# A two-block transformer kernel: a second triangular solve moved into the Fourier tables' place, and a head's work cut into nine pieces between projections

## The chip, the cores and the metric

The kernel is written for Trainium2 and runs on one core of one chip, as one program. The metric is the device time of that program in microseconds (us): the median of three runs. Beside it stands the profile of one execution, taken by the hardware profiler.

The engines meant below are PE (TensorE, matrix products and transposes), ACT (ScalarE), DVE (VectorE), POOL (GpSimd) and SP, the queue that issues nearly all transfers between device memory and on-chip memory. Each works through its own list of instructions in order, and waits at an instruction until what it needs is there.

## What is computed

All data is float32, 1024 tokens of width 1024. A first block (a gated linear recurrence, a short convolution and a pooling branch) hands its output to a second block. That one has a mixer of two branches, then a mixture of 64 experts. The change touches the second block's mixer alone:

```python
proj = rms_norm(h) @ w_in                 # Fourier input, q, k, v, z, a/b, gate_f, gate_d
y_f  = real(fft2(f_in, axes=(1, 3))) @ w_fourier
q, k, v = silu(depthwise_conv(qkv, width 5))       # 8 heads of 128
# per chunk of 64 tokens and head, forward and backward in time:
decay = exp(min(g[:, None] - g[None, :], 0)) on the lower triangle
a_mat = strict_lower((k * beta) @ k.T * decay)
t_mat = inverse(eye + a_mat)                       # triangular solve
qk    = lower(q @ k.T * decay)
# delta rule over the chunks with t_mat, qk, q, k, v and a state per head
y_d   = (rms_norm(o) * silu(z)) @ w_delta
out   = (sigmoid(gate_f) * y_f + sigmoid(gate_d) * y_d) @ w_out
```

## The kernel before, in words

**Products.** A float32 product is made of three passes over values that are split into a high and a low part (`mm3`, whose matmuls stand at lines 195 to 197). A block of weights arrives as `wr` (512 KB); ACT writes its high part `wh` (line 172) and POOL its low part `wl` (line 173).

**Order.** A framework's scheduler makes one ordered list per engine out of the program text; `tc.issue_after(x)` adds that what follows comes behind instruction x on x's engine. Tiles of a pool rotate over `bufs` buffers, so a writer waits until the reader of the buffer's last content is done.

**The heads** (lines 1125 to 1146, from about 1205 us to 1640 us of the profiled execution). For each of 8 heads, `channels` makes one of k, q, v: 72 matmuls for each of three column groups (348, 346, 346), evicted by ACT as `pr` (line 990), a convolution of width 5 on ACT and DVE (lines 994 and 996), then Silu. While head h is projected, head h-1 is finished: `token_rows` transposes k and q on PE (line 1024) and takes their norms on ACT, `value_rows` transposes v, `gram_meta` and `gram` form k k^T and q k^T (line 1093), multiply them by decays and store the results. The decays come from `gb`, cumulative log gates that a transfer copies out of the scratch `GR` to all 128 partitions (line 1003, `decays_in`): DVE subtracts (lines 1069 and 1082), ACT takes the exponent (lines 1071 and 1084). Two buffers in PSUM serve all these transposes (`m`), and two hold `gb` for each direction. The program text has `token_rows` whole behind the first projection and so on; the scheduler interleaves as its own rules have it.

**The tables.** Six loads `tr` (line 1122) bring the discrete Fourier tables, each is split by ACT and POOL (lines 172 and 173) into tiles `th`, `tl`. The text names one per head.

**Fourier and first solve** (1641 to 1773 us). PE transforms while DVE runs the first 38 of 62 steps of the solve of X0 (lines 438 and 440, forward direction, 128 systems of 64x64 side by side).

**Gate loop** (1773 to 1898 us). For n = 0 to 15, PE makes a half of gate_f and of the Fourier branch's output, and DVE multiplies the two (`mul`, line 1282). Between these DVE does the last 24 steps of the first solve, four to a half, in n = 0 to 5. Then ACT turns the solved X0 over (`inverse_out`, line 1208), X1 is loaded into the same place, and its solve (lines 421 and 423) goes on, seven steps to a half, and then alone.

**Tail** (1898 to 2009 us). PE makes six halves of z gates and ten of `gate_d`, 24 matmuls each, evicted by ACT (line 1349 for `gate_d`). When X1 is solved, ACT turns it over as well. Then the pools of the solves are closed, and the delta rule over chunks begins (first matmul at line 1375).

Of the kernel before, what the change touches and what calls it, by code (L numbers as in the profile page):

```python
# [11 lines left out]
F32 = mybir.dt.float32  # L12
# [97 lines left out]
INV0S, INV0 = 38, 6  # L110
# [22 lines left out]
def body(ctx, tc, A):  # L133
# [778 lines left out]
    with ExitStack() as cg:  # L912
# [66 lines left out]
        KQs_, vs_, sks, gbs = {}, {}, {}, {}  # L979

        def channels(h, j, m):

            if j == 0:
                KQs_[h] = pg.tile([P, 2, T2], F32, name="KQ", bufs=2)
            w = w_k if m == 8 else win2.get(512 + m * P)
            pr = pg.tile([P, T2 + 4], F32, name="pr", bufs=2)
            pool_e.memset(pr[:, 0:2], 0.0)
            pool_e.memset(pr[:, T2 + 2:], 0.0)
            for c0, n in CH2:
                act.activation(pr[:, 2 + c0:2 + c0 + n], q_k.pop() if q_k else proj2(w, c0, n), AF.Copy)  # L990
            if j == 2:
# [5 lines left out]
            act.activation(y, y, AF.Silu)  # L997
# [8 lines left out]
        def token_rows(h):  # L1006
# [5 lines left out]
            for j in range(2):  # L1012
# [7 lines left out]
                for gq in range(2):  # L1020
                    q = psm.tile([P, 4, P], F32, name="m")
                    for i in range(4):
                        c = 4 * gq + i
                        pe.transpose(q[:, i, :], KQ[:, j, 16 + c * P:16 + (c + 1) * P], ident)
                    for i in range(4):
                        act.activation(jk, q[:, i, :], AF.Square, accum_out=ss[:, j, 1 + 4 * gq + i:2 + 4 * gq + i])
                    if j == 0:
                        o = pg.tile([P, 4, P], F32, name="kv", bufs=3)
                        act.activation(o, q, AF.Copy)
                        sp.dma_start(KVs[4 * gq:4 * gq + 4, :, h, 0, :].rearrange("c p n -> p c n"), o)  # L1030
            for j in range(2):
                sp.dma_start(KQs[:, :, h, j, :].rearrange("c p t -> p c t"),
                             KQ[:, j, 16:].rearrange("p (c t) -> p c t", t=P))
# [7 lines left out]
            for d_ in range(2):  # L1041
                dve.tensor_mul(bp[:, d_, :, h], beta[:, d_, :, h], rq[:, 0])
                dve.tensor_scalar(nbp[:, d_, :, h], bp[:, d_, :, h], -1.0, None, op0=OP.mult)

        def value_rows(h):
# [6 lines left out]
            for gq in range(2):  # L1052
# [8 lines left out]
                paced[0] = sp.dma_start(KVs[4 * gq:4 * gq + 4, :, h, 1, :].rearrange("c p n -> p c n"), o)  # L1061

# [12 lines left out]
        def gram(h, gq):  # L1075
            KQ, grb = KQs_[h], gbs[h]
            dm = []
            for d_ in range(2):
# [6 lines left out]
                dm.append(t)  # L1085
            at = [pg.tile([P, 4, P], F32, name=f"at{d_}") for d_ in range(2)]
            qt = [pg.tile([P, 4, P], F32, name=f"qt{d_}") for d_ in range(2)]
            for i2 in range(2):
# [5 lines left out]
                for d_ in range(2):  # L1094
                    for i in range(2):
# [5 lines left out]
                                      dm[d_][:, 2 * i2:2 * i2 + 2], op=OP.mult)  # L1101
            cs_ = slice(4 * gq, 4 * gq + 4)
            for d_ in range(2):
# [5 lines left out]
                sp.dma_start(ov, at[d_][0:64, :, 64:128] if d_ == 0 else at[d_][64:128, :, 0:64])  # L1109

        tabs = [[pft.tile([KF, 6, NT], F32R, name=f"t{c}{j}") for c in "hl"] for j in range(2)]
# [13 lines left out]
        for h in range(H + 1):  # L1125
            if 0 < h < H:
                decays_in(h)
            if h < H:
                channels(h, 0, 8 + h)
                table_piece(h) if h < 7 else None  # L1130
            with tc.issue_after(mm[0].ins):
                if h == 0:
                    gates_a()
                else:
                    token_rows(h - 1)
            if h < H:
                channels(h, 1, h)
            if h == 0:
                with tc.issue_after(mm[0].ins):
                    gates_b()  # L1140
                decays_in(0)
            if h:
                value_rows(h - 1)
                gram_meta(h - 1)
                gram(h - 1, 0)
            if h < H:
                channels(h, 2, 16 + h)
            if h:
                gram(h - 1, 1)
# [45 lines left out]
    def inverse_in(d_):  # L1195
        X = pi.tile([P, 64, 64], F32, name="X")
        sp.dma_start(X, N2[d_])
        return X, pi.tile([P, 1024], F32, name="t", bufs=2)
# [61 lines left out]
    cff.close()  # L1260

    with ExitStack() as cf:
# [10 lines left out]
        for d in range(KT):  # L1273
            wg = win2.get(4640 + d * P)
            wp = wfo.get(d * P)
            for half, tt in enumerate(HALF):
# [9 lines left out]
                with tc.issue_after(mul.ins):  # L1286
                    if n < INV0:
                        run(solve, -(-(62 - INV0S) // INV0))
                    if n == INV0 - 1:
                        ones(X0)  # L1290
                    if n > INV0:
                        run(solve, 7)
                if n == INV0:
                    with tc.issue_after(sent.ins), tc.issue_after(gate.ins):
                        inverse_out(0, X0)
                        X1_, t1_ = inverse_in(1)
                    solve = solve_lower(X1_, 64, t1_)
    run(solve)
    ones(X1_)
    for h in range(5, H):  # L1300
        z_gate(h)
        if h == 6:
            with tc.issue_after(gated[0].ins):
                inverse_out(1, X1_)
            cpi.close()
# [865 lines left out]
```

## Time and profile before

| | us |
|---|---|
| three runs | 3086.24, 3081.46, 3084.51 |
| median | 3084.51 |
| the profiled execution, its own time | 3079.72 |
| its span in the trace | 3078.0 |
| PE busy | 2795.7 (91%) |
| DVE, ACT, POOL busy | 1518.6, 1051.5, 881.1 |

Times inside the trace are counted from the span's start. An engine's busy time is not yet its cost: what matters is where PE, the busiest engine, stands idle or runs at a lower clock, and which instruction ends each such pause. "Idle before, releaser" in the rows says how long an engine stood before an instruction and what let it go on.

### The profile page before, as it was taken

What the parts mean: (1) busy time and instruction counts of PE and PEld (TensorE: products, weight loads), DVE (VectorE), ACT (ScalarE), POOL (GpSimd) and SP (SyncE); (2) the same over time, 40 slices, a digit from 0 to 9 for tenths busy, and PEclk for the clock granted to TensorE, in tenths of its full rate; (3) what the DMA queues carried; (4) which work ended last, traced back from release to release, by engine and by line L of the source; (5) the groups of instructions that cost most, each with busy time, mean ns of one, the idle gap of its engine ahead of it and who ended that gap; (6) DMA issues with size and microseconds to landing.
All of it is one profiled execution on the core that took longest, in us unless ns stands there. A gap on an engine that the chain in (4) does not pass through costs nothing.

```text
span 3078.0 us, 42949 instructions
## 1 busy us (share of the span) xinstructions
PE 2795.7 (91%) x16109; PEld 2239.5 (73%) x16109; DVE 1518.6 (49%) x2484; ACT 1051.5 (34%) x2060; POOL 881.1 (29%) x703
## 2 busy tenths in 40 slices
PE   7999989999999997699999999889999986888884
PEld 6777877888788786698898778679888763545442
DVE  3343993323411434565578968833564442222226
ACT  4444112223312344477683231234543210111112
POOL 1233233222333452111115832222475310111011
PEclk9999999999999999899999999989999988999997
DMA  4456415444344444466553343399988569999996
GB/s 117 120 141 197 160 42 149 146 138 123 95 124 158 127 149 105 96 150 138 139 158 107 99 142 102 118 275 263 275 244 292 203 242 400 405 407 409 394 376 268
DMA packets 532931, 599.79 MB, mean 195 GB/s; under 512 B 120784, under 2 KB 429188, under 8 KB 512368
## 3 DMA queue, kind: packets, MB, share of 16 engines
q1 hardware_dynamic: 525808, 582.60, 58.8%
q0 software_dynamic: 6912, 14.41, 1.2%
q8 instruction: 128, 2.10, 0.3%
q14 instruction: 83, 0.68, 0.1%
HBM read 473.23 MB, written 134.44 MB: 197 GB/s over the span
## 4 chain that ended last, share of the span: by engine, by line
PE 56%; DMA 20%; DVE 14%; POOL 3%; issue 3%; ACT 3%; SPq 1%; ACTq 0%; DVEq 0%; POOLq 0%
PE q L197 12%; PE q L196 11%; PE q L195 11%; PE q L1838 5%; DMA wr<-in_w_gate_e_dram 4%; DMA gb<-GR 3%; DVE X L440 2%; DMA yl<-in_w_gate_e_dram 2%; DVE X L423 2%; DVE t L421 2%; DVE t L438 2%; DMA g<-in_w_gate_e_dram 1%; DMA t<-GF 1%; PE g L405 1%; DMA d<-in_w_down_e_dram 1%
## 5 line engine op out<-in xcount | busy, mean ns | idle before, releaser
L173 POOL TENSOR_TENSOR wl<-wr,wh 128x1024 fp32r<-128x1024 f32 x142 | 355.7, 2505 | 737.6 <-ACT wh L172 729.8
L196 PE MATMUL q<-hTh,wl 128*128 128x512 f32 x1040 | 412.7, 397 | 7.9 <-POOL wl L173 7.9
L195 PE MATMUL q<-hTh,wh 128*128 128x512 f32 x1040 | 416.6, 401 | 2.2 <-DVE t L824 1.4
L197 PE MATMUL q<-hTl,wh 128*128 128x512 f32 x1040 | 417.5, 401 | 0.0
L195 PE MATMUL q<-h2h,wh 128*128 128x346 f32 (+4 forms) x1080 | 387.0, 358 | 2.3 <-DVE h2l L780 1.9
L196 PE MATMUL q<-h2h,wl 128*128 128x346 f32 (+4 forms) x1080 | 385.0, 356 | 1.8 <-POOL wl L173 1.8
L197 PE MATMUL q<-h2l,wh 128*128 128x346 f32 (+4 forms) x1080 | 385.2, 357 | 0.0
L196 PEld LDWEIGHTS q<-hTh,wl 128*128 128x128 f32 x1040 | 196.7, 189 | 57.8 <-POOL wl L173 9.4
L195 PEld LDWEIGHTS q<-hTh,wh 128*128 128x128 f32 x1040 | 197.1, 190 | 50.1 <-issue 5.8
L197 PEld LDWEIGHTS q<-hTl,wh 128*128 128x128 f32 x1040 | 196.8, 189 | 46.6 <-issue 3.9
L195 PEld LDWEIGHTS q<-h2h,wh 128*128 128x128 f32 (+1 forms) x1080 | 207.9, 192 | 22.4 <-DVE h2l L780 2.5
L196 PEld LDWEIGHTS q<-h2h,wl 128*128 128x128 f32 (+1 forms) x1080 | 207.4, 192 | 20.2 <-POOL wl L173 2.1
L197 PEld LDWEIGHTS q<-h2l,wh 128*128 128x128 f32 (+1 forms) x1080 | 208.1, 193 | 18.4
L172 ACT ACTIVATE wh<-wr 128x1024 fp32r<-128x1024 f32 x142 | 148.4, 1046 | 38.9 <-PE q L197 19.9
L438 DVE TENSOR_TENSOR t<-X 128x62 f32<-128x62 f32 (+30 forms) x124 | 155.3, 1252 | 11.2 <-DMA br<-in_w_branch_dram 7.6
L440 DVE TENSOR_TENSOR X<-X,t 128x62 f32<-128x62 f32 (+30 forms) x124 | 152.3, 1228 | 3.4
L1819 POOL DMA_INDIRECT xg<-HN,gidx x28 | 28.6, 1023 | 376.2 <-PE t L1832 316.2
L1838 PE MATMUL q<-yl,xT 128*32 128x256 f32 (+2 forms) x416 | 109.7, 427 | 26.5 <-DMA yl<-in_w_gate_e_dram 26.2
L1840 ACT ACTIVATE sg<-q 128x256 f32<-128x256 f32 x28 | 10.7, 383 | 328.1 <-PE q L1838 328.1
L1838 PE MATMUL q<-mh,xT 128*64 128x256 f32 (+2 forms) x416 | 108.4, 421 | 11.6 <-DMA mh<-in_w_gate_e_dram 11.4
L1841 DVE TENSOR_TENSOR sg<-sg,q 128x256 f32<-128x256 f32 x28 | 11.8, 420 | 216.0 <-ACT sg L1840 216.0
L1838 PE MATMUL q<-g,xT 128*32 128x256 f32 (+2 forms) x400 | 93.1, 464 | 22.8 <-DMA g<-in_w_gate_e_dram 20.9
(629 smaller groups left out, 5943.2 us busy)
## 6 DMA issues: line engine op xcount, KB each, us to landing
wr<-in_w_in_dram SPq DMA_DIRECT2D x125, 512.0 KB
d<-in_w_down_e_dram SPq DMA_DIRECT2D x38, 1024.0 KB
g<-in_w_gate_e_dram SPq DMA_DIRECT2D x25, 1024.0 KB
u<-in_w_up_e_dram SPq DMA_DIRECT2D x25, 1024.0 KB
KQ<-KQs SPq DMA_DIRECT2D x32, 512.0 KB
KV<-KVs SPq DMA_DIRECT2D x32, 512.0 KB
wr<-in_w_gate_e_dram SPq DMA_DIRECT2D x26, 512.0 KB
mh<-in_w_gate_e_dram SPq DMA_DIRECT2D x13, 1024.0 KB
```

The lines of the kernel that those rows point to most:

```text
L172: act.activation(hi, src, AF.Copy)
L173: pool_e.tensor_sub(lo, src, hi.bitcast(F32))
L195: pe.matmul(out, sh(k), mh(k), start=(k == 0), stop=False)
L196: pe.matmul(out, sl(k), mh(k), start=False, stop=False)
L197: mm[0] = pe.matmul(out, sh(k), ml(k), start=False, stop=(k == kt - 1))
L405: pe.matmul(q[:, i, :], BK[hs, 4 * g + i].rearrange("p a t -> p (a t)"), AR[hs, 4 * g + i].rearrange("p a t -> p (a t)"), start=True, stop ...
L421: dve.tensor_tensor(t, X[:, s + 1:n, s:s + 1].to_broadcast([X.shape[0], m, s]), X[:, s:s + 1, 0:s].to_broadcast([X.shape[0], m, s]), op=OP ...
L423: dve.tensor_add(X[:, s + 1:n, 0:s], X[:, s + 1:n, 0:s], t)
L438: dve.tensor_tensor(t, X[:, 0:s, s:s + 1].to_broadcast([X.shape[0], s, m]), X[:, s:s + 1, s + 1:n].to_broadcast([X.shape[0], s, m]), op=OP ...
L440: dve.tensor_add(X[:, 0:s, s + 1:n], X[:, 0:s, s + 1:n], t)
L1819: nc.gpsimd.indirect_dma_start(out=xg, out_offset=None, in_=HN, in_offset=bass.IndirectOffsetOnAxis(ap=gi, axis=0), bounds_check=S - 1, oo ...
L1838: up[0] = pe.matmul(qs[r_, j], xT[:, k, r_], w[j][k], start=(k == 0), stop=(k == 7))
```

## The change

1. **Second solve.** X1 and its scratch rows now lie where the Fourier tables lay (`tab`, one tile in place of four). X1's load stands right behind the last Fourier table matmul. In the gate loop the first solve gets eight steps to a half in n = 0 to 2, and the second five to a half from n = 3 on. The first solved matrix is turned over from n = 4, the second after the z gates of head 5 rather than 6.
2. **Nine pieces.** The work that finishes head h-1 is a generator with nine stops, and one piece is placed behind the first matmul of each of the nine column groups of head h. The decay matrices are formed a piece ahead of the Gram products. `decays_in` stands at the end of a head's iteration.
3. **Tables.** One table piece per head, from the second head on, behind that head's first Silu and behind the last transposed store of the head before.

```diff
-INV0S, INV0 = 38, 6
+INV0S, INV0 = 38, 2
...
-        def channels(h, j, m):
+        def channels(h, j, m, pieces):
...
             for c0, n in CH2:
                 act.activation(pr[:, 2 + c0:2 + c0 + n], q_k.pop() if q_k else proj2(w, c0, n), AF.Copy)
+                with tc.issue_after(mm[0].ins):
+                    next(pieces, None)
...
+        def head(h):
+            yield from token_rows(h)
+            dm0 = decay_matrices(h, 0)
+            yield from value_rows(h)
+            gram_meta(h)
+            yield
+            dm1 = decay_matrices(h, 1)
+            yield from gram(h, 0, dm0)
+            yield from gram(h, 1, dm1)
...
-        tabs = [[pft.tile([KF, 6, NT], F32R, name=f"t{c}{j}") for c in "hl"] for j in range(2)]
+        tab = pft.tile([P, 24, NT], F32, name="tab")
+        tabs = [[tab[:KF, 12 * j + 6 * i:12 * j + 6 * i + 6, :].bitcast(F32R) for i in range(2)] for j in range(2)]
...
-        for h in range(H + 1):
-            if 0 < h < H:
-                decays_in(h)
-            if h < H:
-                channels(h, 0, 8 + h)
-                table_piece(h) if h < 7 else None
...
+        for h in range(H):
+            pieces = head(h - 1) if h else chain(iter([None] * 2), gates())
+            channels(h, 0, 8 + h, pieces)
+            if h and h < 8:
+                with tc.issue_after(silus[0].ins), tc.issue_after(paced[0].ins):
+                    table_piece(h - 1)
+            channels(h, 1, h, pieces)
+            channels(h, 2, 16 + h, pieces)
+            run(pieces)
+            decays_in(h)
+        run(head(H - 1))
...
+        else:
+            X = pft.tile([P, 24, NT], F32, name="tab").rearrange("p k t -> p (k t)")
+            X, t = X[:, 0:4096].rearrange("p (s t) -> p s t", t=64), X[:, 4096:5120]
         sp.dma_start(X, N2[d_])
...
     cff.close()
+    X1_, t1_ = inverse_in(1)
+    solve1 = solve_lower(X1_, 64, t1_)
...
                 with tc.issue_after(mul.ins):
-                    if n < INV0:
-                        run(solve, -(-(62 - INV0S) // INV0))
-                    if n == INV0 - 1:
+                    run(solve, 8)
+                    if n == INV0:
                         ones(X0)
                     if n > INV0:
-                        run(solve, 7)
-                if n == INV0:
+                        run(solve1, 5)
+                if n == INV0 + 2:
                     with tc.issue_after(sent.ins), tc.issue_after(gate.ins):
                         inverse_out(0, X0)
-                        X1_, t1_ = inverse_in(1)
-                    solve = solve_lower(X1_, 64, t1_)
-    run(solve)
+    run(solve1)
     ones(X1_)
     for h in range(5, H):
         z_gate(h)
-        if h == 6:
+        if h == 5:
             with tc.issue_after(gated[0].ins):
                 inverse_out(1, X1_)
-            cpi.close()
+    cpi.close()
```

ACT's list where the heads begin, as one piece of the difference (`v` is the evicted a/b projection, `tr` a table, `nea` a gate constant, `pr` a projection's eviction):

```order
 L917 ACTIVATE v<-q 32x348
-L990 ACTIVATE pr<-q 128x348
-L172 ACTIVATE th_8971<-tr 87x524
+L991 ACTIVATE pr<-q 128x348
 L937 ACT_TABLE_LOAD
 L937 ACTIVATE nea<-nea 128x16
-L172 ACTIVATE th_8971<-tr 87x524 x2
-L917 ACTIVATE v<-q 32x346
-L172 ACTIVATE th_8973<-tr 87x524 x2
-L917 ACTIVATE v<-q 32x346
-L172 ACTIVATE wh<-wr 128x1024
-L172 ACTIVATE th_8973<-tr 87x524
```

The six table splits stood among and ahead of the two evictions `v`; now none stands here, and both evictions follow `nea` directly.

SP's list around the loads of `gb` in a middle head, before:

```order
L1109 DMA OFF<-at_10216 64x4x64
L1003 DMA gb_10716<-GR 128x9x128
L1003 DMA gb_10718<-GR 128x9x128
L184 DMA wr<-in_w_in_dram 128x8x128
L1019 DMA KV_8888<-kv 16x128
L184 DMA wr<-in_w_in_dram 128x8x128
```

and now:

```order
L1122 DMA OFF<-at_10172 64x4x64
L1022 DMA KV_8888<-kv 16x128
L1033 DMA KVs<-kv 128x4x128
L184 DMA wr<-in_w_in_dram 128x8x128
L1006 DMA gb_11176<-GR 128x9x128
L1006 DMA gb_11178<-GR 128x9x128
L1033 DMA KVs<-kv 128x4x128
```

The pair of loads came right behind the last store of the Gram products; now two stores of the next head's transposed k and a load of weights stand between.

ACT's list in the tail, before (`z` is a half of a gate, line 1208 the turning over of X1):

```order
L172 ACTIVATE wh<-wr 128x1024
L1349 ACTIVATE z<-q 128x512 x2
L172 ACTIVATE wh<-wr 128x1024
L1208 ACTIVATE t<-X 128x1024 x2
L1349 ACTIVATE z<-q 128x512
L1208 ACTIVATE t<-X 128x1024
L1349 ACTIVATE z<-q 128x512
```

and now (line 1231 turns over X1, which lies in `tab`):

```order
L1371 ACTIVATE z<-q 128x512 x2
L172 ACTIVATE wh<-wr 128x1024
L1231 ACTIVATE t<-tab 128x1024 x2
L1371 ACTIVATE z<-q 128x512 x2
L172 ACTIVATE wh<-wr 128x1024
L1231 ACTIVATE t<-tab 128x1024 x2
L1371 ACTIVATE z<-q 128x512 x2
```

Before, 14 of the tail's 16 halves were evicted ahead of the first turning over; now 8 are (six of z, two of `gate_d`), and eight follow.

## Rows read from the trace of the kernel before

**Rows 1.** The page: busy time by engine, and the chain by engine.

```profile
PE 2795.7 (91%) x16109; PEld 2239.5 (73%) x16109; DVE 1518.6 (49%) x2484; ACT 1051.5 (34%) x2060; POOL 881.1 (29%) x703
...
PE 56%; DMA 20%; DVE 14%; POOL 3%; issue 3%; ACT 3%; SPq 1%; ACTq 0%; DVEq 0%; POOLq 0%
```

**Rows 2.** Busy time by stretch: us, each engine, clock, DMA share.

```profile
core 0: us, PE busy (x) PEld busy (x) DVE busy (x) ACT busy (x) POOL busy (x), PEclk, DMA share, GB/s
...
1831.00:1854.00 23.00, 23.00 (x102) 18.70 (x101) 3.08 (x9) 12.63 (x11) 7.31 (x4) 1.00 0.93 341
...
1989.00:2009.00 20.00, 0.00 (x0) 0.00 (x0) 1.21 (x3) 9.44 (x7) 3.27 (x4) 0.57 0.98 306
2009.00:2050.00 41.00, 37.35 (x277) 33.45 (x278) 12.20 (x36) 14.55 (x48) 7.80 (x11) 0.80 0.99 286
```

**Rows 3.** ACT's timeline, heads' begin: start, us, instruction, idle before.

```profile
1224.56 0.64 ACT L172 ACTIVATE th<-tr 87x524 fp32r<-87x524 f32 x1 [3.58 <-DMA tr<-in_dft_dram]
...
1231.31 0.64 ACT L172 ACTIVATE th<-tr 87x524 fp32r<-87x524 f32 x1 [3.58 <-DMA tr<-in_dft_dram]
1231.86 0.43 ACT L917 ACTIVATE v<-q 32x346 f32<-32x346 f32 x1
```

**Rows 4.** PE's timeline of the same stretch.

```profile
1225.59 0.53 PE L929 MATMUL m<-ident,v 32*128 32x32 f32 x3 [4.35 <-ACT v L917]
1232.34 0.53 PE L929 MATMUL m<-ident,v 32*128 32x32 f32 x3 [6.22 <-ACT v L917]
...
1235.72 0.66 PE L196 MATMUL q<-h2h,wl 128*128 128x348 f32 x1 [1.77 <-POOL wl L173]
```

**Rows 5.** The chain of waits, 1200 to 1350 us: start, us, what.

```profile
1264.09 9.77 DMA gb<-GR
...
1283.71 20.47 DMA gb<-GR
...
1335.49 11.42 DMA gb<-GR
```

**Rows 6.** A middle head: DVE's timeline.

```profile
1346.94 0.22 DVE L1069 SCALAR_TENSOR_TENSOR dmm<-gb,gc,C 16x16 f32<-16x16 f32 x1 [8.27 <-DMA gb<-GR]
```

**Rows 7.** Line 1069 on DVE, 1300 to 1600 us: idle until (us, times).

```profile
  DMA gb<-GR: 51.7, 6
```

**Rows 8.** A middle head: PE's timeline.

```profile
1349.15 0.66 PE L1024 MATMUL m<-ident,KQ 128*128 128x128 f32 x4 [3.34 <-ACT kv L1018]
```

**Rows 9.** Groups of instructions, 1340 to 1525 us (four heads).

```profile
L1024 PE MATMUL m<-ident,KQ 128*128 128x128 f32 x64 | 10.8, 296 | 14.1 <-ACT kv L1018 14.1
```

**Rows 10.** Busy time by stretch, columns of rows 2: four heads.

```profile
1340.00:1525.00 185.00, 170.61 (x1035) 164.90 (x1033) 113.96 (x252) 133.09 (x308) 30.19 (x35) 0.95 0.62 145
```

**Rows 11.** DVE's timeline, end of Fourier and first product.

```profile
1768.49 3.21 DVE L440 TENSOR_TENSOR X<-X,t 128x950 f32<-128x950 f32 x1
1780.16 0.69 DVE L1282 TENSOR_TENSOR t<-t,q 128x512 f32<-128x512 f32 x1 [8.46 <-PE q L197]
```

**Rows 12.** DVE's timeline in the tail: second solve.

```profile
1938.88 1.16 DVE L423 TENSOR_TENSOR X<-X,t 128x962 f32<-128x962 f32 x1
...
1941.26 1.15 DVE L423 TENSOR_TENSOR X<-X,t 128x950 f32<-128x950 f32 x1
...
1989.02 0.27 DVE L423 TENSOR_TENSOR X<-X,t 128x62 f32<-128x62 f32 x1
```

**Rows 13.** POOL's groups, 1773 to 1990 us.

```profile
L173 POOL TENSOR_TENSOR wl<-wr,wh 128x1024 fp32r<-128x1024 f32 x15 | 41.7, 2779 | 145.0 <-ACT wh L172 145.0
```

**Rows 14.** PE's timeline: gate loop's end, chunks' start.

```profile
1897.55 0.39 PE L195 MATMUL q<-h2h,wh 128*128 128x512 f32 x1
...
2009.12 1.86 PE L1375 MATMUL v<-KV,tm 16*16 16x128 f32 x8 [22.46 <-DMA KV<-KV]
```

**Rows 15.** ACT's timeline in the tail.

```profile
1989.33 3.76 ACT L1208 ACTIVATE t<-X 128x1024 f32<-128x1024 f32 x2 [12.14 <-DVE X L423]
```

**Rows 16.** SP's queue in the tail.

```profile
2003.45 0.79 SPq L1368 DMA_DIRECT2D tm<-TM  x1
```

More of the change, by code (lines that the diff above doesn't have):

```diff
@@ L975, in gates_b @@
                 sp.dma_start(GR[d_], gr)
-        KQs_, vs_, sks, gbs = {}, {}, {}, {}
-        def channels(h, j, m):
+        KQs_, vs_, sks, gbs, silus = {}, {}, {}, {}, [None]
+        def channels(h, j, m, pieces):
             if j == 0:
@@ L996, in channels @@
                 dve.scalar_tensor_tensor(y, pr[:, i:i + T2], cw2[:, i, m:m + 1], y, op0=OP.mult, op1=OP.add)
-            act.activation(y, y, AF.Silu)
+            silus[0] = act.activation(y, y, AF.Silu)
         def decays_in(h):
@@ L1030, in token_rows @@
                         sp.dma_start(KVs[4 * gq:4 * gq + 4, :, h, 0, :].rearrange("c p n -> p c n"), o)
+                    if (j, gq) != (1, 1):
+                        yield
             for j in range(2):
@@ L1043, in token_rows @@
                 dve.tensor_scalar(nbp[:, d_, :, h], bp[:, d_, :, h], -1.0, None, op0=OP.mult)
+            yield
         def value_rows(h):
@@ L1061, in value_rows @@
                 paced[0] = sp.dma_start(KVs[4 * gq:4 * gq + 4, :, h, 1, :].rearrange("c p n -> p c n"), o)
+                if gq == 0:
+                    yield
         def gram_meta(h):
@@ L1073, in gram_meta, with decay_matrices @@
             sp.dma_start(NM[h], dm)
-        def gram(h, gq):
-            KQ, grb = KQs_[h], gbs[h]
-            dm = []
+        def decay_matrices(h, gq):
+            grb, dm = gbs[h], []
             for d_ in range(2):
@@ L1085, in gram @@
                 dm.append(t)
+            return dm
+        def gram(h, gq, dm):
+            KQ = KQs_[h]
             at = [pg.tile([P, 4, P], F32, name=f"at{d_}") for d_ in range(2)]
@@ L1101, in gram @@
                                       dm[d_][:, 2 * i2:2 * i2 + 2], op=OP.mult)
+                if i2 < gq:
+                    yield
             cs_ = slice(4 * gq, 4 * gq + 4)
@@ L1109, in gram, with gates @@
                 sp.dma_start(ov, at[d_][0:64, :, 64:128] if d_ == 0 else at[d_][64:128, :, 0:64])
-        tabs = [[pft.tile([KF, 6, NT], F32R, name=f"t{c}{j}") for c in "hl"] for j in range(2)]
+            if gq == 0:
+                yield
+        def head(h):
[3 more added lines that the diff above has]
+            gram_meta(h)
+            yield
+            dm1 = decay_matrices(h, 1)
+            yield from gram(h, 0, dm0)
+            yield from gram(h, 1, dm1)
+        def gates():
+            gates_a()
+            for _ in range(3):
+                yield
+            gates_b()
+        tab = pft.tile([P, 24, NT], F32, name="tab")
+        tabs = [[tab[:KF, 12 * j + 6 * i:12 * j + 6 * i + 6, :].bitcast(F32R) for i in range(2)] for j in range(2)]
         raws = []
@@ L1123, in table_piece @@
                 raws.append((r, j, k))
-        for h in range(H + 1):
-            if 0 < h < H:
-                decays_in(h)
-            if h < H:
-                channels(h, 0, 8 + h)
-                table_piece(h) if h < 7 else None
[L1131 to L1149, printed above, removed]
+        for h in range(H):
[9 more added lines that the diff above has]
+        run(head(H - 1))
     FM = scratch("FM", (512, S))
@@ L1195, in inverse_in @@
     def inverse_in(d_):
-        X = pi.tile([P, 64, 64], F32, name="X")
+        if d_ == 0:
+            X, t = pi.tile([P, 64, 64], F32, name="X"), pi.tile([P, 1024], F32, name="t", bufs=2)
+        else:
+            X = pft.tile([P, 24, NT], F32, name="tab").rearrange("p k t -> p (k t)")
+            X, t = X[:, 0:4096].rearrange("p (s t) -> p s t", t=64), X[:, 4096:5120]
         sp.dma_start(X, N2[d_])
-        return X, pi.tile([P, 1024], F32, name="t", bufs=2)
+        return X, t
     def ones(X):
```

## Prediction, made before the changed kernel ran

> **What bounds the kernel now.** The page is read first: PE is busy for 91% of the span, and the chain that ended last lies on PE for 56% and on transfers for 20% [rows 1]. So the time is PE's work, plus the places where PE stands still or runs at the lower clock; everything else is cover. The second view, busy time by stretch, shows where those places are in the part that the change touches: the reader is to see that PE did nothing from 1989 to 2009 us and ran at 0.80 of its clock behind that, while DVE had been idle for most of 1831 to 1854 us [rows 2]. The third view, the timelines, says what ended each pause. Three stages matter, and each has its own limit: the start of the heads (table splits on ACT), the middle heads (the `gb` transfer), and the stretch from the gate loop to the first chunk (DVE's second solve). The rest of block 1, the chunks and the experts only move along.
>
> The sum is made against the profiled execution, 3079.7 us. The median of the runs is 4.8 us above that, and I add these 4.8 at the end. About 0.2% (6 us) is what a measurement of this kernel can tell from no change.
>
> **Start of the heads: 11 us.** ACT waits at table splits for `tr`, 3.58 us each time, and the evictions `v` stand behind them in its list [rows 3]. PE's next transposes wait for these evictions: 4.35 and 6.22 us [rows 4]. ACT's new list has no table split here. Nothing else is late in their place: the gate constant `nea`, which is still ahead of the evictions, was there before the second split. So 4.35 + 6.22 = 10.6, taken as 11 with some of the lower clock behind the gaps. The wait of 1.77 us for `wl` [rows 4] stays, as ACT's and POOL's split of that weight block still comes after the eviction. Bounds: 8 (a later `wr` or `nea` takes some of it back) and 14.
>
> Behind it comes a chain of two `gb` transfers, 9.77 and 20.47 us [rows 5]. The change keeps its instructions and their order, so it starts earlier and costs the same: nothing gained, nothing lost.
>
> **Middle heads: 9 us.** A head's small decay `dmm` reads `gb`, and the scheduler has put it early in DVE's list. DVE stood 8.27 us for the transfer [rows 6], one of six such waits that make 51.7 us [rows 7]; the transfer took 11.42 us in the chain [rows 5]; ACT waits for `dmm`, and PE for the transposes' buffer behind ACT, 3.34 us [rows 8]. Over four heads PE lost 14.1 us in this group [rows 9], 3.5 a head. The mean clock of these 185 us is 0.95 [rows 10]; the missing 0.05 is 9.3 us, 2.3 a head. So a head costs 5.8 us beyond PE's work, and five heads have this wait, as the first of DVE's six belongs to the chain above: 29 us is all that could be won. Now SP issues the pair of `gb` loads three transfers later (two stores of the transposed k and a load of weights), which works against the gain. For it speaks that `dmm`'s exponent also stands later in ACT's list, behind an eviction, a weight split, the first four k norms and a scaling, and that the transposes are spread over nine places, so that a late buffer stops PE for less. The pause thus gets shorter, but doesn't go. Neither end has a row; I take a third, 9 us, and keep 0 and 29. The pieces add no instruction to PE. What they move onto ACT is six table splits of 0.64 us [rows 3], one to a head: hidden beside PE's matmuls as long as ACT has room, and it is busy for 133 of the 185 us [rows 10]. If that room were gone they would cost 4 us in all.
>
> **Fourier stage: minus 1 us.** X1's load (2 MB) goes out behind the last table matmul, ahead of the store and loads of FM for which PE waits before the first product at 1780.16 us [rows 11]. At the 341 GB/s of 1831 to 1854 us [rows 2], in which X1 was loaded before, 2.1 MB are 6.2 us: bounds 0 and 6.2. The load has been on its way for a while when the stores and loads of FM are issued, and I take 1. DVE's own wait of 8.46 us [rows 11] is one for PE, and stays.
>
> **Gate loop and tail: 14 us.** DVE is the limit here. In 1831 to 1854 us it worked 3.08 of 23 us [rows 2], as X1 could not be loaded before X0 was turned over in its place. With a place of its own X1 goes on without that pause: the last step at 1989.02 us [rows 12] would come 19.9 us earlier, at 1969. Its steps are the same, in the same number.
>
> Against that stands POOL. A solve step of 950 elements took 3.21 us while POOL worked [rows 11], and 1.15 us without [rows 12]. In DVE's pause POOL ran four splits, 7.31 us [rows 2]; now they meet working steps, each of which can lengthen by 3.21 - 1.15 = 2.06 us. Between 0 and 8.2 us, I take 3, as not every split meets a long step: X1 solved at 1972. The Trainium skill, "SBUF — State Buffer", section "Who interferes with whom", says that GpSimd and VectorE lock the ports they share for a whole instruction, and that the other one is blocked fully. By that all 7.3 us would be added, and the sum would be 4 less; the row agrees in kind, since the extra 2.06 us is most of one POOL split of 2.78 us [rows 13].
>
> What does PE make of it? In six halves DVE now has 11 to 14 solve instructions ahead of the product, and PE may be two halves ahead of the products (four PSUM buffers, two to a half). The last product comes with 51 solve instructions left; in the trace the last 51 began at 1938.88, 50.4 us before the end [rows 12]. So it comes at 1972 - 50 = 1922, the one two halves before at about 1902, and PE ends the gate loop near 1905.5 instead of 1897.55 [rows 14]: 8 us later. Then 16 halves of 24 matmuls follow, which took 2009.12 - 22.46 - 1897.55 = 89 us [rows 14], 5.56 each. ACT evicts eight of them, up to 1950 us, and then stands at the turning over of X1 until 1972 us; the first two copies take 3.76 us [rows 15]. PE can be four halves ahead, up to 1972, so it pauses for about 4 us and loses 2 more to the clock, as in a middle head. The first chunk's matmul stands behind 15 halves in PE's new list: 1905.5 + 83.4 + 6 = 1995, against 2009.12 [rows 14]: 14 us. The 16th half, 5.6 us, now lies among the chunks' first instructions, and I count 5 of it as added. In return the chunks' loads, issued no earlier than 2003.45 us before [rows 16], can go out by about 1986, and PE comes to them after matmuls rather than after a pause of 22.46 us. The lower clock of 2009 to 2050 us cost 41 x 0.20 = 8.2 us [rows 2]; I take 5 of that back. 14 - 5 + 5 = 14. Bounds: 0 (DVE or ACT takes it all) and 22.5, the whole pause, plus 8.
>
> **Sum.** 11 + 9 - 1 + 14 = 33: 3079.7 - 33 = 3046.7, and on the median's scale **3051 us**. With its own bounds this case covers 3034 to 3068.
>
> **The rivals.**
> *The heads keep their pause.* The three transfers ahead of `gb` on SP cost what the later `dmm` wins, and the tail gives half: 11 + 0 - 1 + 7 = 17, thus 3067, down to 6 us of gain. For it: SP's new list. Chance 0.20.
> *The heads run clear.* `gb` arrives in time: 14 + 29 + 20 = 63, thus 3021. For it: in the heads without `dmm` PE has no such pause; against it: the later issue. Chance 0.10.
> *Slower: `gb` becomes the heads' clock.* Its loads now share the queue with two stores, weights and a table. If each took 20.47 us, as one did where several transfers were queued [rows 5], instead of 11.42, each of five heads would lose 9.05 more: 45 against 11 - 1 + 14 = 24 won, thus 3106. It decides from a load of 11.42 + 24/5 = 16.2 us on. Against it: 20.47 was the second of four such loads issued together. Chance 0.07.
> *No change that can be told.* ACT, which evicts in order behind pieces, splits and three kinds of function, makes each of seven heads 3 us longer, and the tail gives only a few: 11 - 21 + 8 = -2, thus 3086. For it: ACT's 133 us in 185 [rows 10] leave 13 us of room a head, but it waits in order. Chance 0.08.
>
> **How the numbers follow.** The forecast has 0.55. Faster takes in it and the first two rivals: 0.85; no change 0.08; slower 0.07. The range leaves out the last two rivals and the far part of the clear heads: 3024 to 3078.
>
> **What would show it.** Right: no PE gap for `v` near 1225 us; a gap of 1 to 3 us a head at the k transposes, where it was 3.34; DVE without a pause between its two solves; ACT waiting some 20 us at the first copy out of `tab`; the first chunk matmul about 33 us earlier on the trace's scale (19 from the stages before it, 14 from its own). Wrong: `gb` landing later in a head than before, DVE standing longer for it; PE pausing inside the gate loop for products by more than 8 us; or the first chunk's matmul waiting for its loads still.

## The result, and the profile after

The changed kernel takes 3045.97 us (median of 4 runs, 3043.69 to 3049.41); the kernel before took 3082.99 us in the same comparison (4 runs, 3079.28 to 3086.24). The ratio is 0.9881, 95% interval 0.9864 to 0.9898: 37 us faster, where 33 were forecast and 3051 us. A second comparison gave 0.9914 (0.9894 to 0.9935). The total came out nearly as forecast. Its terms did not: the middle heads were forecast 17 us too well, and the other terms together 14 us too badly.

The page of the changed kernel, its busy line and its chain by engine, which answer to [rows 1]:

```profile
PE 2786.0 (91%) x16109; PEld 2230.2 (73%) x16109; DVE 1508.4 (49%) x2484; ACT 1051.6 (35%) x2061; POOL 887.8 (29%) x703
...
DMA 11%; PE 8%; DVE 1%; ACT 1%; issue 0%; POOL 0%; SPq 0%; ACTq 0%; DVEq 0%; POOLq 0%
```

PE's work is the same number of instructions in a shorter span. The second row can't be set beside that of before: its shares add up to 21%, and the page's lines of this chain are nearly all the experts', so it was followed back through the span's end only.

**Where the time went.** The same projection matmul can be found in both traces by counting them; the difference of its start times is what has been won up to there.

| place | before, us | after, us | won up to there |
|---|---|---|---|
| last projection of block 2's first pieces | 1215.1 | 1215.3 | 0 |
| start of the heads done | 1249.3 | 1233.2 | 16 |
| both first `gb` transfers done | 1334.3 | 1316.0 | 18 |
| end of the heads | 1632.4 | 1622.1 | 10 |
| first projection of the gate loop | 1779.9 | 1765.7 | 14 |
| among the tail's gate halves | 1944.8 | 1931.5 | 13 |
| among the chunks | 2089.8 | 2060.9 | 29 |
| end of the span | 3078.0 | 3047.6 | 30 |

So the start of the heads won 16, the chain behind it 2, the middle heads **lost** 8, the Fourier stage won 4, gate loop and tail 15, and what lies behind 1 more. Two traces of one and the same kernel differ by up to 5 us at these places (`e0_before` below), so the small terms are known to a few us only. The profiled execution took 3049.41 us, 30 less than that of before; the medians are 37 apart.

*Start of the heads.* Busy time by stretch, columns as in [rows 2]:

```profile
1205.00:1225.00 20.00, 20.00 (x125) 16.95 (x124) 2.48 (x7) 7.24 (x11) 4.72 (x2) 0.94 0.44 38
1225.00:1250.00 25.00, 25.00 (x162) 24.91 (x162) 19.36 (x32) 17.16 (x28) 4.44 (x7) 1.00 0.31 87
```

Before, the second of these stretches read:

```profile
1225.00:1250.00 25.00, 15.99 (x83) 15.36 (x84) 16.04 (x24) 13.80 (x23) 9.94 (x8) 0.69 0.24 67
```

PE has no pause at all in these 45 us. The waits of 4.35, 6.22 and 1.77 us [rows 4] are gone, and the clock is at 0.94 and 1.00, where the second stretch had 0.69.

*First `gb` transfers.* PE's waits from 1245 to 1310 us (what waited, for what, us in all, times, longest):

```profile
PE m L1054 <- ACT jk L1029: 11.7, 1, 11.7
PE m L1027 <- DVE gr L974: 5.9, 1, 5.9
```

17.6 us; it is the same chain as in [rows 5], come earlier.

*Middle heads.* PE's waits from 1320 to 1500 us, four heads, to be set beside [rows 9]:

```profile
PE m L1054 <- ACT jk L1029: 17.2, 4, 5.2
PE m L1062 <- ACT jk L1029: 2.2, 4, 0.6
```

The pause did not shrink. It moved from the k transposes to the v transposes, and grew from 14.1 to 19.4 us (16.4 in a second trace of the changed kernel, `e9_after`). The mean clock of four heads fell as well, from 0.95 [rows 10] to 0.92 in these 180 us. On SP's queue (start, us on the queue, what) one sees what stands ahead of `gb`:

```profile
1367.27 0.61 SPq L1122 DMA_DIRECT2D OFF<-at  x1
1367.98 0.55 SPq L1022 DMA_DIRECT2D KV<-kv  x1
1368.63 0.37 SPq L1033 DMA_DIRECT2D KVs<-kv  x1
1369.09 0.46 SPq L184 DMA_DIRECT2D wr<-in_w_in_dram  x1
1369.64 2.41 SPq L1006 DMA_DIRECT2D gb<-GR  x2
```

and on DVE what `dmm` waited for it, 10.86 us against 8.27 in [rows 6]:

```profile
1381.61 0.22 DVE L1077 SCALAR_TENSOR_TENSOR dmm<-gb,gc,C 16x16 f32<-16x16 f32 x1 [10.86 <-DMA gb<-GR]
```

*Gate loop and tail.* By stretch, columns as in [rows 2]:

```profile
1831.00:1854.00 23.00, 23.00 (x101) 18.73 (x101) 22.76 (x31) 8.74 (x7) 4.81 (x2) 1.00 0.48 174
...
1975.00:2020.00 45.00, 38.68 (x294) 34.23 (x293) 10.43 (x32) 16.66 (x51) 12.10 (x12) 0.89 0.97 275
```

DVE worked 22.76 of the 23 us in which it had worked 3.08. ACT's timeline shows X1 solved at 1947.9, 41 us earlier than in [rows 12]:

```profile
1929.48 1.05 ACT L172 ACTIVATE wh<-wr 128x1024 fp32r<-128x1024 f32 x1
1947.95 3.94 ACT L1231 ACTIVATE t<-tab 128x1024 f32<-128x1024 f32 x2 [17.41 <-DVE tab L423]
1951.80 1.06 ACT L1371 ACTIVATE z<-q 128x512 f32<-128x512 f32 x2
```

ACT waited 17.41 us there, where the prediction had some 20. The first chunk's matmul comes right behind other matmuls, 33.7 us earlier than in [rows 14]:

```profile
1975.45 1.04 PE L1397 MATMUL v<-KV,tm 16*16 16x128 f32 x8
```

The 22.46 us pause of [rows 14] is gone. PE's waits from 1900 to 2060 us are:

```profile
PE pk L1453 <- DVE X L1456: 4.4, 1, 4.4
PE q L195 <- ACT wh L172: 2.7, 1, 2.7
PE v L1437 <- DMA OF<-OFF: 1.9, 1, 1.9
PE q L196 <- POOL wl L173: 1.9, 1, 1.9
```

2.7 and 1.9 us, for a weight split that stands behind the copies on ACT, are what the solve still costs PE; the two others lie in the chunks, where the kernel before had 3.5 us of waits beside its long pause. No wait of PE stands in the gate loop.

### The profile page after: what moved, and what is told of

Read it like the earlier page. It is cut to its first block, busy times and chain, and to the rows that moved or that the text cites. A ratio compares the mean times of both kernels' runs of the same rounds, so it can differ in the third digit from the quotient of the medians.

```text
span 3047.6 us, 42939 instructions
## 1 busy us (share of the span) xinstructions
PE 2786.0 (91%) x16109; PEld 2230.2 (73%) x16109; DVE 1508.4 (49%) x2484; ACT 1051.6 (35%) x2061; POOL 887.8 (29%) x703
## 5 line engine op out<-in xcount | busy, mean ns | idle before, releaser
L173 POOL TENSOR_TENSOR wl<-wr,wh 128x1024 fp32r<-128x1024 f32 x142 | 364.4, 2567 | 663.3 <-ACT wh L172 640.3
L440 DVE TENSOR_TENSOR X<-X,t 128x62 f32<-128x62 f32 (+30 forms) x124 | 158.5, 1279 | 2.8
```

The lines of the kernel that those rows point to most:

```text
L173: pool_e.tensor_sub(lo, src, hi.bitcast(F32))
L440: dve.tensor_add(X[:, 0:s, s + 1:n], X[:, 0:s, s + 1:n], t)
```

## The experiments

All times are medians, each compared with runs of the kernel before on the same chip: 3072.02 us for `e1` to `e4`, 3076.33 for `e0` and `e5` to `e7`, 3072.78 for `e8` to `e11`. The table gives, from the traces, what each kernel had won at five places against the kernel before's own trace from the second of these comparisons (`e0_before`), by the same matmul; negative means later.

| kernel | start of heads | `gb` chain | end of heads | gate loop's start | among the chunks |
|---|---|---|---|---|---|
| changed kernel | 15 | 17 | 6 | 12 | 26 |
| e1_pin | 13 | 20 | 40 | 42 | 60 |
| e2_tables | 15 | 15 | 8 | 8 | 8 |
| e3_solve | 0 | 0 | -1 | 5 | 21 |
| e4_pieces | 0 | 0 | -8 | -4 | -4 |
| e5_nosolve | 13 | 14 | 5 | 7 | 10 |
| e6_pin_before | -1 | 6 | 31 | 32 | 34 |
| e7_nopieces | 14 | 22 | 45 | 52 | 68 |
| e8_gbfirst | 15 | 14 | 4 | 8 | 26 |
| e10_gr | 14 | 21 | 44 | 49 | 65 |

The first trace of the kernel before lies up to 5 us behind `e0_before` at these places; differences of a few us between traces mean nothing by themselves. An "edge" below is one use of `tc.issue_after`.

### e1_pin: what `dmm` costs

```diff
-                dve.tensor_scalar(nbp[:, d_, :, h], bp[:, d_, :, h], -1.0, None, op0=OP.mult)
+                nbs[0] = dve.tensor_scalar(nbp[:, d_, :, h], bp[:, d_, :, h], -1.0, None, op0=OP.mult)
...
-            dve.scalar_tensor_tensor(dm, gb[:16, 0, :16], gc[:16, 0, 0, h:h + 1],
-                                     con2("dmf")[:16, :16], op0=OP.subtract, op1=OP.min)
+            with tc.issue_after(nbs[0].ins):
+                dve.scalar_tensor_tensor(dm, gb[:16, 0, :16], gc[:16, 0, 0, h:h + 1],
+                                         con2("dmf")[:16, :16], op0=OP.subtract, op1=OP.min)
```

> The changed kernel with one order edge added: the small decay dmm of a head is put behind that head's own q-norm factors on VectorE. Theory A (in the middle heads the time goes to the hoisted dmm, which waits for a gb load that is needed only a head later): ScalarE's wait for dmm, 38.0 us in 7, falls below 5 us, PE's waits at the v transposes (17.2 us in four heads) go, and with the clock behind them 30 to 45 us are won: about 3000 to 3016. Theory B (gb is late for whatever reads it first): the wait moves to the decay matrices dm, PE still stands 3 us or more a head, and under 10 us are won: above 3036.

Measured: 3009.08 us, 0.9796 of the kernel before (0.9774 to 0.9818), 63 us faster than it; the changed kernel, not run beside it, had won 37 and 26. PE's waits in the same stretch of the trace as above, 1320 to 1500 us:

```profile
PE m L1062 <- ACT jk L1029: 1.1, 1, 1.1
PE m L1054 <- ACT jk L1029: 0.7, 1, 0.7
```

1.8 us where there were 19.4. Theory A holds. The load of `gb` is not too late for the decay matrices: they no longer hold PE. `dmm` of a head whose turn comes a head later was put in front of work that was due.

### e2_tables, e3_solve, e4_pieces, e5_nosolve: the parts alone

The paced tables alone:

```diff
-                table_piece(h) if h < 7 else None
+                if h:
+                    with tc.issue_after(silus[0].ins), tc.issue_after(paced[0].ins):
+                        table_piece(h - 1)
```

> The kernel before, with the tables paced one to a head and nothing else. Theory A (the start of the heads pays for six table splits, and a split inside a head is hidden): 16 us at the start, which stay to the end: 3064 to 3070. Theory B (the table splits cost in the heads what they cost at the start): 3076 or more.

Measured: 3068.11 us, 0.9986 (0.9975 to 0.9997), 4 us faster. The time lies in theory A's range, but that was reckoned from the kernel before's 3083, and it took 3072 here; as a difference 4 us fits theory B better. The trace shows both halves: 15 us won at the start, 7 of them lost again by the end of the heads. PE's waits from 1320 to 1500 us:

```profile
PE m L1024 <- ACT kv L1018: 17.6, 4, 4.9
PE m L1056 <- ACT kv L1050: 1.9, 4, 0.6
```

That is 17.6 us where [rows 9] has 14.1. A table piece inside a head is not free in this version.

The second solve alone (all of the diff's hunks on `INV0`, `tab`, `inverse_in`, the gate loop and the turning over, on the kernel before):

> The kernel before, with the second solve in the place of the tables, begun sooner, and nothing else. Theory A (the tail was one wait for VectorE's second solve): first chunk 20 us earlier, 17 to 22 us in all: 3061 to 3066. Theory B (part of the gain of the tail comes from the heads' new order, through transfers or PSUM): under 12 us: above 3071.

Measured: 3051.15 us, 0.9932 (0.9909 to 0.9955), 21 us faster, with 5 won before the gate loop and 16 in the tail. Theory A, by its difference: the solve part's gain does not need the rest.

The nine pieces alone (the changed kernel with the solve hunks undone and the tables named as before):

> The kernel before, with the nine pieces and the later place of the gb loads in the text, tables and solve as before. Theory A (the new order of the heads costs 1.5 to 2 us a head, as the gb loads leave later behind two stores and weights, and dmm waits longer): 3088 to 3096. Theory B (the pieces themselves win, and the loss in the heads is that of the tables): 3076 or less.

Measured: 3080.88 us, 1.0033 (1.0022 to 1.0044), 9 us slower. In the trace it loses 8 us by the end of the heads, 1.6 for each of five. Theory A by its difference; its time was again reckoned from 3083.

Pieces and paced tables together:

```diff
-            table_piece(h) if h < 7 else None
+            if h and h < 8:
+                with tc.issue_after(silus[0].ins), tc.issue_after(paced[0].ins):
+                    table_piece(h - 1)
```

(against `e4_pieces`)

> The changed kernel with its solve part undone: nine pieces and paced tables alone. Theory A (the parts add up): tables alone won 4 us, pieces alone lost 9, so 3 to 7 us slower than before. Theory B (pieces and tables need each other: a table split between whole blocks of transposes delays them, between pieces it does not): 10 to 18 us faster than before, as the whole change less the 21 us that the solve part won alone.

Measured: 3065.39 us, 0.9961 (0.9947 to 0.9975), 11 us faster: with the 21 us of the solve part that makes 32, and the whole change won 37 and, in a second comparison, 26. The parts don't add up, and the reason given in theory B is not what the traces show. Tables alone lost 7 us in the heads, pieces alone 8, and both together also 8 to 9. The loss of the one does not come on top of that of the other: a table piece costs 1.5 us a head where the pieces are missing, and 0.2 beside them (periods in the table below). Why they don't add is open.

### e6_pin_before, e7_nopieces: is it the pieces?

The same edge on the kernel before, and nothing else:

> The kernel before with the one order edge on dmm and nothing else. Theory A (the hoisted dmm is the whole of the heads' pause, with pieces or without): PE's 14.1 us in four heads and the clock behind them go, 25 to 40 us faster. Theory B (only the spread transposes give ScalarE the room): under 12 us faster.

Measured: 3042.46 us, 0.9886 (0.9869 to 0.9902), 34 us faster with one order edge. The group that had 14.1 us of waiting in [rows 9] has none (instructions, busy and mean, idle before), theory A:

```profile
L1024 PE MATMUL m<-ident,KQ 128*128 128x128 f32 x72 | 10.8, 272 | 0.0
```

Tables, solve and the edge, without the pieces:

> Paced tables, the second solve and the edge on dmm, without the nine pieces. Theory A (pieces add nothing once dmm is pinned): 58 to 68 us faster than before, as much as with pieces (63). Theory B (pieces are worth the loss that they took where dmm was not pinned): 45 to 55 us faster.

Measured: 3007.08 us, 0.9774 (0.9758 to 0.9790), 69 us faster, 1 above theory A's range: pieces add nothing once `dmm` is in its place. Here the parts do add up: 34 for the edge (`e6_pin_before`), 15 at the start of the heads for the tables, 21 for the solve (`e3_solve`) make 70. Behind the start's chain this version wins 23 us by the end of the heads, `e6_pin_before` 25, so with the edge six table pieces cost next to nothing there. By stretch, 1300 to 1550 us:

```profile
1300.00:1550.00 250.00, 248.66 (x1575) 241.90 (x1574) 171.94 (x379) 197.94 (x464) 53.61 (x60) 1.00 0.69 167
```

PE is busy for 248.66 of 250 us at full clock. The heads have nearly no pause left.

### e8_gbfirst, e9_after: why the heads lost, and didn't win

With the three parts of a head's period read from the traces (last `dm` of a head to the issue of `gb`; issue to the end of `dmm`; `dmm` to the next last `dm`; the mean of four or five heads):

| kernel | to the issue | load, to `dmm` | to the next last `dm` | period |
|---|---|---|---|---|
| e0_before | 0.8 | 11.5 | 33.8 | 46.1 |
| e2_tables | 2.0 | 11.3 | 34.3 | 47.6 |
| e4_pieces | 4.2 | 12.4 | 30.9 | 47.5 |
| changed kernel | 4.0 | 12.7 | 31.0 | 47.7 |
| e9_after | 4.3 | 12.2 | 31.4 | 47.9 |
| e8_gbfirst | 2.4 | 11.5 | 33.9 | 47.8 |

The period is a closed loop. `gb`'s buffer comes free with the last `dm`, the load goes out, `dmm` waits for it, ACT and PE wait for `dmm`, and the next last `dm` waits for them. What is put into one of the three parts adds to the period unless another part gives way, and an engine's share of busy time does not tell which it will be. With the pieces the third part is 2.8 us shorter and the first two are 4.4 longer: 3.2 up to the issue and 1.2 in the load. Of the 3.2, the three transfers ahead of `gb` took 1.7 (on SP's queue above, from 1367.98 to 1369.64 us; the same in all five heads). The other 1.5 are the last head's own Gram products: one store of them was still to be sent behind the last `dm` before, two to four now. `e2_tables` has the same at 1.2 us.

`e9_after` is the changed kernel again. `e8_gbfirst` puts the loads ahead of these transfers:

```diff
         def head(h):
+            dm0 = decay_matrices(h, 0)
+            dm1 = decay_matrices(h, 1)
+            if h + 2 < H:
+                decays_in(h + 2)
             yield from token_rows(h)
-            dm0 = decay_matrices(h, 0)
...
-                    sp.dma_start(KV0[:, h, 0, :], o[:16, 0])
+                    with tc.issue_after(gl[0].ins):
+                        sp.dma_start(KV0[:, h, 0, :], o[:16, 0])
...
             run(pieces)
-            decays_in(h)
+            if h < 2:
+                decays_in(h)
```

> The changed kernel again, as a reference on the chip of the runs beside it: 0.9881 of the kernel before, within 0.003, so about 37 us faster.

Measured: 3046.57 us, 0.9914 (0.9894 to 0.9935), 26 us faster; the interval of the first comparison was 0.9864 to 0.9898, which it barely meets. The expectation, 0.9881 within 0.003, was missed by a hair.

> The changed kernel, with a head's gb loads put ahead of the next head's stores of transposed k on SP (the decay matrices are written ahead of the transposes in the text, so that this is possible); dmm stays where the scheduler puts it. Theory A (a head's period is a loop of three parts: from the last dm to the issue of gb, 0.8 us before and 3 to 4.8 now; the load, 11.5 before and 12.7 now; from dmm to the next last dm, 33.8 before and 31.0 now): the first part goes back to about 1 us and the period from 47.3 to 43 to 44.5 us, so 12 to 20 us faster than the changed kernel. Theory B (SP's order is not what holds the heads): within 4 us of the changed kernel.

Measured: 3049.07 us, 0.9933 (0.9909 to 0.9958), no change against `e9_after`. The number is theory B's. The table shows that theory A's first step came true (4.3 to 2.4 us, and the load 0.7 shorter), and that the third part took it all back: 31.4 to 33.9. ACT's timeline says why. With the load earlier, the scheduler put `dmm` earlier, too. In `e9_after`:

```profile
1373.55 0.44 ACT L991 ACTIVATE pr<-q 128x346 f32<-128x346 f32 x1
1373.89 1.05 ACT L172 ACTIVATE wh<-wr 128x1024 fp32r<-128x1024 f32 x1
1374.84 0.27 ACT L1029 ACTIVATE jk<-m 128x128 f32<-128x128 f32 x1
...
1375.09 1.17 ACT L997 ACTIVATE KQ<-pr,cw 128x1040 f32<-128x1040 f32 x1
...
1382.78 0.21 ACT L1079 ACTIVATE dmm<-dmm 16x16 f32<-16x16 f32 x1 [5.22 <-DVE dmm L1077]
1382.90 0.25 ACT L1029 ACTIVATE jk<-m 128x128 f32<-128x128 f32 x1
```

In `e8_gbfirst`:

```profile
1381.13 0.22 ACT L1080 ACTIVATE dmm<-dmm 16x16 f32<-16x16 f32 x1 [4.77 <-DVE dmm L1078]
1381.26 0.43 ACT L991 ACTIVATE pr<-q 128x346 f32<-128x346 f32 x1
1381.60 1.04 ACT L172 ACTIVATE wh<-wr 128x1024 fp32r<-128x1024 f32 x1
1382.54 0.25 ACT L1030 ACTIVATE jk<-m 128x128 f32<-128x128 f32 x1
...
1382.79 1.15 ACT L997 ACTIVATE KQ<-pr,cw 128x1040 f32<-128x1040 f32 x1
```

An eviction (`pr`), a weight split (`wh`), a k norm (`jk`) and a scaling (`KQ`) stand ahead of the waiting exponent (`dmm`) in the one, and behind it in the other. PE gets its buffer 1.3 us after the exponent in the first (starting at 1384.09):

```profile
1384.09 0.38 PE L1054 MATMUL m<-ident,v 128*16 128x128 f32 x1 [3.38 <-ACT jk L1029]
```

and 3.9 us after it in the second (1385.04):

```profile
1385.04 0.38 PE L1055 MATMUL m<-ident,v 128*16 128x128 f32 x1 [2.94 <-ACT jk L1030]
```

An earlier load is of no use as long as the scheduler answers by having its reader wait earlier.

### e10_gr, e11_nopieces: the start's own chain

> Paced tables, the second solve and the edge on dmm, without the nine pieces, again beside the others: 0.977 of the kernel before, 30 to 36 us faster than the changed kernel.

Measured: 3007.23 us, 0.9791 (0.9771 to 0.9810), 39 us faster than the changed kernel beside it. This version beats both kernels.

`e10_gr` adds to it an edge on the decay matrices in the first head:

```diff
-                dve.tensor_copy(gr, q)
+                grs[0] = dve.tensor_copy(gr, q)
...
-                    dve.scalar_tensor_tensor(t[:, i], grb[d_][:, c, :], gc[:, d_, c, h:h + 1],
-                                             con2("dmf" if d_ == 0 else "dmb"), op0=OP.subtract, op1=OP.min)
+                    with tc.issue_after(grs[0].ins):
+                        dve.scalar_tensor_tensor(t[:, i], grb[d_][:, c, :], gc[:, d_, c, h:h + 1],
+                                                 con2("dmf" if d_ == 0 else "dmb"), op0=OP.subtract, op1=OP.min)
```

> As e11_nopieces, and the decay matrices dm put behind the second copy gr on VectorE, which starts the second direction's way through GR to gb. Theory A (in the first head the copy stood behind a dm that waits 6.5 us for the first direction's gb): the second load leaves some 9 us earlier, PE's 8.6 us pause at line 1024 goes, and 6 to 11 us are won over e11_nopieces. Theory B (the second load then only queues behind the first and its weights): under 3 us.

Measured: 3005.59 us, 0.9781 (0.9760 to 0.9803): the same as without it. DVE's copy did come ahead of the `dm` that it had stood behind (1253.76 against 1257.79 in `e11_nopieces`, though this trace runs 3 us later),

```profile
1253.76 0.28 DVE L976 COPY gr<-m 72x128 f32<-72x128 f32 x1
```

but on SP's queue the store of it stood behind a load of weights until 1257.52 and then took 5.54 us to go out (2.22 in `e11_nopieces`), and the second load left at 1267.89, no sooner than in `e11_nopieces` (1265.54):

```profile
1250.73 1.01 SPq L1005 DMA_DIRECT2D gb<-GR  x2
1252.60 4.82 SPq L184 DMA_DIRECT2D wr<-in_w_in_dram  x1
1257.52 5.54 SPq L977 DMA_DIRECT2D GR<-gr  x1
1267.89 11.70 SPq L1005 DMA_DIRECT2D gb<-GR  x3
```

Theory B, by its number: the second way through `GR` queues behind the first loads and the weights. Why the store itself took 5.54 us was not tried. PE's longest pause there shrank from 9.1 to 6.6 us and did not go.

`e0_before` is the kernel before, run once more for its trace.

> The kernel before itself, for a trace from the chip of the runs beside it. Theory: its stages end up to the first chunk as in the first trace of it, within 3 us; what differs between chips lies in the experts.

It took 3079.83 us. Its stages lie within 5 us of the first trace's, not within 3.

## Why the prediction was right in the sum and wrong in its terms

**Start of the heads (11; measured 16).** The cause was right. The step that failed is "the wait of 1.77 us for `wl` stays": that wait is gone, too, and so is one of 0.4 us for `wh`, as the splits no longer stand ahead of `wh` on ACT and of `wl` on POOL. The four waits make 12.8 us. The rest of the 16 fits the clock, which stood at 0.69 from 1225 to 1250 us and now at 1.00.

**First `gb` chain (0; measured 2).** PE's waits fell from 20.2 us (6.07 and 13.29 among them) to 17.6.

**Middle heads (9 won; measured 8 lost).** The step that failed is "the pause thus gets shorter". Both effects that it weighed are real, and the table of the loop gives them their sizes: the later place of `dmm`'s exponent and the spread transposes won 2.8 us a head; against it, `gb` went out 3.2 us later and its load took 1.2 longer. Only 1.7 of the 3.2 are the three transfers that the prediction named; the rest, the stores of the Gram products, it did not see. It called the transfers a counterweight, took a third of the gain and bounded it by 0 from below. There was no reason for that bound. Its own sign of being wrong, DVE standing longer for `gb`, came true (10.86 us for 8.27). That `dmm`'s early place makes the pause is shown by the edge, with the pieces (`e1_pin`) and without (`e6_pin_before`); the split of the loss is read from traces, and `e8_gbfirst`, which moved the three transfers behind, won nothing. The rival "the heads keep their pause" said that the transfers cost what the later `dmm` wins, and stood closest here. The "29 us is all that could be won" was about right: `e6_pin_before` won 25 behind the start's chain. But it was to be had by an order edge, not by this change. The table splits were "hidden beside PE's matmuls as long as ACT has room" in the prediction, by ACT's share of busy time. In this change that held: the period is 47.5 us without paced tables (`e4_pieces`) and 47.7 with them. It does not hold by itself: without the pieces (`e2_tables`) a table piece costs 1.5 us a head, 1.2 of it up to the issue of `gb` on SP's queue and 0.5 in the third part. There ACT's share of busy time would have misled.

**Fourier stage (1 lost; measured 4 won on PE).** The load of X1 delayed nothing that mattered. The first product itself came 10.5 us earlier, as much as the end of the heads, and DVE waited 6.47 us for it where [rows 11] has 8.46:

```profile
1769.70 0.69 DVE L1307 TENSOR_TENSOR t<-t,q 128x512 f32<-128x512 f32 x1 [6.47 <-PE q L197]
```

So the 4 us are PE's alone. `e3_solve` wins 6 us between the end of the heads and this place, but `e4_pieces`, which leaves the solves as they were, wins 4; where they come from stays open.

**Gate loop and tail (14; measured 15).** The mechanism held: X1 goes on where DVE had been idle. Its sub-terms were off. From the first product to X1's last step DVE took 1989.3 - 1780.2 = 209.1 us before and 1947.9 - 1769.7 = 178.2 now: 30.9 less, where 19.9 less 3 were forecast. The idle 19.8 us are gone. "I take 3" for POOL's splits is a step that failed: 18 solve instructions of this stretch took over 1.35 us before and 19 now, so the splits met hardly more of them, and the instructions took 175.0 us in all before and 172.1 now. The Trainium skill's rule of the locked ports ("SBUF — State Buffer", "Who interferes with whom": one of GpSimd and VectorE waits for the whole of the other's instruction) would, as the prediction estimated, have added 7.3; these traces show the long instructions, but hardly more of them. The rest of the 30.9, some 8 us, is for the most part in how the two solves alternate; the last section shows it. "8 us later" at the end of the gate loop did not come: PE has no wait there. So the tail was forecast with DVE too slow and PE too late: the first chunk's matmul came 33.7 us earlier, 19.5 by this stage's doing, where 14 were forecast. And the chunks' start was forecast too cheap: by the place among the chunks 5 of these us are lost again, where the sum had 5 lost to the 16th half and 5 won back from the clock. The errors offset each other; that the first chunk came 33.7 us earlier for a forecast of 33 is luck as well. PE paused 4.6 us behind ACT where 4 were forecast.

**The sum.** 16 + 2 - 8 + 4 + 15 + 1 = 30 in the profiled executions, against the 33 forecast. The 17 us too many in the heads were nearly made good by terms that were too small: 5 at the start, 2 in the `gb` chain, 5 in the Fourier stage, 1 in the tail and 1 behind it. The total was right in part by luck. The range of 3034 to 3068 was narrower than the prediction's own bounds, which add up to between 2 and 74 us won.

## What to carry to other kernels

When an instruction waits on a transfer whose buffer is freed by the same loop, ask first who put it so early: one order edge on a 16x16 subtraction was worth as much as this whole change. A cost that stands inside such a loop can add to the period even where its engine has room (1.5 us a head in `e2_tables`), and cost next to nothing once the loop is broken (`e7_nopieces`); read the loop's parts from issue to issue before calling anything hidden. And a sum that agrees with the measurement is no proof of its terms: compare them stage by stage.

## What had not been expected of the hardware

Two solves that take turns on DVE run faster than one alone. In the kernel before, a solve's instruction starts 0.03 us after the end of the one whose result it reads (156 neighbours in the gate loop and the tail, 0.034 us on average). DVE's timeline there, start and duration first:

```profile
1804.31 0.98 DVE L438 TENSOR_TENSOR t<-X 128x782 f32<-128x782 f32 x1
1805.32 0.97 DVE L440 TENSOR_TENSOR X<-X,t 128x782 f32<-128x782 f32 x1
1806.32 0.94 DVE L438 TENSOR_TENSOR t<-X 128x752 f32<-128x752 f32 x1
```

In the changed kernel's gate loop, where steps of X0 (lines 438 and 440) and X1 (lines 421 and 423) alternate, the next one starts before the end of the last (67 neighbours, 0.077 us on average):

```profile
1811.54 0.74 DVE L438 TENSOR_TENSOR t<-X 128x572 f32<-128x572 f32 x1
1812.20 0.65 DVE L421 TENSOR_TENSOR tab<-tab 128x486 f32<-128x486 f32 x1
1812.78 0.74 DVE L440 TENSOR_TENSOR X<-X,t 128x572 f32<-128x572 f32 x1
1813.44 0.65 DVE L423 TENSOR_TENSOR tab<-tab 128x486 f32<-128x486 f32 x1
```

That is 0.11 us each, 7.4 us for the 67. The trace of the kernel before shows the same overlap, 0.08 us, at the 25 places where a gate's product stands beside a solve step, so it is not a matter of the two solves: in these traces it goes with an instruction that does not read the last one's result. It was not tried by itself.

The three comparisons of the experiments ran on three chips; the median of the kernel before was 3072.02, 3076.33 and 3072.78 us in them, and 3082.99 in the comparison of the result. Whether the chip makes that difference was not tried. The changed kernel's ratio was 0.9881 in one comparison and 0.9914 in another, and their intervals overlap by only 0.0004: a difference of a few us between kernels should be measured side by side.
